# Feed-forward gate/up pairs as 2x2 block products with seven products, and SBUF handed out by phase

## The chip, the cores and the metric

The kernel runs on one core of one Trainium2 chip. The metric is the device time of one execution in microseconds (us). In the rows, PE is TensorE's matmuls and PEld its weight loads, DVE is VectorE, ACT ScalarE, POOL GpSimd, and SP SyncE, which issues the DMAs. In the code they are T, V, A, G and SP.

## The reference

Two layers of an encoder on 512 tokens of width 1024, float32. Each layer mixes the tokens in four ways, merges the four by gates, projects, adds the residual and normalises; then comes a feed-forward network of width 2816 (22 tiles of 128):

```python
for l in range(DEPTH):                       # DEPTH = 2
    h = x @ w_in[l]                          # q, k, v, gates of four token mixers
    ...                                      # retention, attention, GLA, S5 -> branches
    mixed = sum(sigmoid(x @ w_gate[l, b] + b_gate[l, b]) * (branches[b] @ w_branch[l, b]) for b in range(4))
    x = _layer_norm(DEEPNORM_ALPHA * x + mixed @ w_out[l], ln1_g[l], ln1_b[l])
    ffn = (silu(x @ w_ffn_gate[l]) * (x @ w_ffn_up[l])) @ w_ffn_down[l]
    x = _layer_norm(DEEPNORM_ALPHA * x + ffn, ln2_g[l], ln2_b[l])
```

## The kernel before

Every float32 product is made of three matmuls in the float32r type. `split` writes a value as a high part (a cast on ACT) and a low part (a subtraction on DVE), and `three` pairs high with high, high with low, low with high. The activations lie transposed in SBUF as XH and XL (128 partitions x 8 slices of the width x 512 tokens). A weight tile is loaded by SP into a ring `wr` of two buffers (`wload`) and split into the rings `wh` and `wl` of three.

In the gate/up stage `gemm_t` makes one tile of 128 outputs for all 512 tokens: 2 halves of 256 tokens x 3 pairs x 8 slices = 48 matmuls with 256 columns. Each of the 22 steps f makes a gate tile and an up tile, then silu on ACT, their product on DVE, and a split of that product g, which stays in SBUF for the down projection. `proj_ln` multiplies such split operands with the rows of a weight matrix, by 4 blocks t of 128 tokens, into eight PSUM banks, and calls `layer_norm` for each block as it becomes complete. `layer_norm` takes its square root as a power on POOL. Its `rest()` transposes a block on PE, applies scale and shift out of PSUM (ACT; DVE for half of the last block), and splits the result into XH and XL; the `rest()` of the last block is called inside the next stage's first matmuls (`late`). Its `rows()` applies scale and shift to the untransposed block on POOL, for the residual of the next normalisation.

Small tiles of 128x512 come from one pool: 53 slots of tag "a", 7 of "sg", 8 of "acc" (`BUFS`). PSUM has rings of 3 (`mm`) and 5 banks (`mx`). During layer 0's gate/up stage the state tables of layer 1's S5 mixer are also made (`s5_constants` on DVE, ACT and POOL, `s5_table` on POOL), and stored to DRAM (`esp`).

The order of the mixers' work is written by a planner (`Pace`, `run`) with costs of its own. The order of all instructions on each engine is made when the kernel is built, by priority (the order in the text, loads' splits ahead) and by when operands and buffers become free; on the chip each engine then works its list in order.

## Time and profile before

| | |
|---|---|
| time, 3 runs | median 1721.31 us (1719.19 to 1741.71) |
| profiled execution | 1720.08 us, span of instructions 1717.9 us |
| PE busy | 1651.2 us (96%) |
| DVE / ACT / POOL busy | 1000.2 / 613.4 / 353.4 us |
| gate/up stage, layer 0 and 1 | 499.8 to 748.4 us, 1343.3 to 1587.8 us |
| down projection of layer 0, to layer 1's start | 748.4 to 871.2 us |
| mean granted TensorE clock | 0.983 |

Shares of the span are means over stages with different limits, so a change in one stage is read from that stage's windows. Matmuls overlap: their cost is the distance of their starts, not the duration that a row shows. The time of the profiled execution holds some 2 us before the first and after the last instruction.

### The profile page before, as it was taken

To read this page: it belongs to the slowest core of one execution; us is meant where nothing else is said; L and a number is where in the kernel's file an instruction comes from. 1 tells how busy PE (TensorE), PEld (TensorE's weight loads), DVE (VectorE), ACT (ScalarE), POOL (GpSimd) and SP (SyncE) were. 2 spreads that over 40 slices of the span, in tenths; PEclk is the share of its full clock that TensorE was granted. 3 is DMA by queue.
4 is the path that set the end of the run, shared out by engine and by line. 5 is a ranking of instruction groups with operands and counts; after the bars stand their busy time and mean duration, and the time that the engine had idled before them with its cause. 6 is when DMAs were issued, how large, how long until landed. Compare 5 with 4: busy or idle time off the path is not lost. (4 is left out here: it accounts for less than half of the span.)

```text
span 1717.9 us, 27806 instructions
## 1 busy us (share of the span) xinstructions
PE 1651.2 (96%) x11596; PEld 1531.0 (89%) x11596; DVE 1000.2 (58%) x1473; ACT 613.4 (36%) x1012; POOL 353.4 (21%) x363
## 2 busy tenths in 40 slices
PE   8999998889999999999999999999999999999997
PEld 7989898779889999988889898988898899999886
DVE  4666579987586533322374665789865833333226
ACT  4454532233343222221154545433342522222112
POOL 0601024560038921000060000122300600000002
PEclk9998999899999999999999999999999999999999
DMA  6532212222433333322327332233324232222232
GB/s 200 176 111 76 86 62 94 82 82 99 141 99 99 123 123 117 119 98 98 111 74 259 104 96 92 64 117 125 125 93 160 86 102 96 99 99 99 98 99 74
DMA packets 66205, 186.94 MB, mean 109 GB/s; under 512 B 7136, under 2 KB 7328, under 8 KB 66080
## 3 DMA queue, kind: packets, MB, share of 16 engines
q1 hardware_dynamic: 66080, 185.17, 32.7%
q8 instruction: 91, 1.49, 0.4%
q14 instruction: 34, 0.28, 0.0%
HBM read 170.46 MB, written 14.68 MB: 108 GB/s over the span
## 5 line engine op out<-in xcount | busy, mean ns | idle before, releaser
L121 DVE TENSOR_TENSOR wl<-wr,wh 128x1024 fp32r<-128x1024 f32 (+2 forms) x250 | 317.3, 1270 | 440.9 <-ACT wh L121 427.0
L121 ACT CAST wh<-wr 128x1024 fp32r<-128x1024 f32 (+2 forms) x250 | 257.5, 1032 | 671.1 <-PE pg L121 223.6
L121 PE MATMUL pg<-XH,wh 128*128 128x256 f32 x2432 | 337.4, 281 | 2.2 <-DVE fs L121 2.2
L121 PE MATMUL pg<-XL,wh 128*128 128x256 f32 x2432 | 333.8, 280 | 2.5 <-DVE XL L121 2.5
L121 PE MATMUL pg<-XH,wl 128*128 128x256 f32 x2432 | 333.0, 280 | 0.0
L121 PEld LDWEIGHTS pg<-XH,wh 128*128 128x128 f32 x2432 | 312.1, 192 | 8.1 <-issue 3.1
L121 PEld LDWEIGHTS pg<-XL,wh 128*128 128x128 f32 x2432 | 306.0, 191 | 3.3 <-DVE XL L121 3.3
L121 PEld LDWEIGHTS pg<-XH,wl 128*128 128x128 f32 x2432 | 305.9, 191 | 0.4
L121 POOL TENSOR_TENSOR rs<-ve,ct 128x1 f32<-128x1 f32 x16 | 10.9, 682 | 718.2 <-DVE ve L121 718.2
L121 DVE TENSOR_TENSOR fs<-fs,pg 128x512 f32<-128x512 f32 x44 | 30.2, 687 | 159.5 <-PE pg L121 159.5
L121 PE MATMUL pj<-wl,gh 128*128 128x512 f32 x320 | 102.3, 393 | 0.0
L121 PE MATMUL pj<-wh,gl 128*128 128x512 f32 x320 | 101.8, 391 | 0.0
L121 PE MATMUL pj<-wh,gh 128*128 128x512 f32 x320 | 101.7, 391 | 0.0
L121 POOL TENSOR_TENSOR acc<-acc,sg 128x512 f32<-128x512 f32 x32 | 61.6, 1929 | 170.3 <-DVE sg L121 170.3
L121 PEld LDWEIGHTS pj<-wh,gh 128*128 128x128 f32 x320 | 59.9, 188 | 13.5
L121 PEld LDWEIGHTS pj<-wl,gh 128*128 128x128 f32 x320 | 60.1, 188 | 13.1
L121 PEld LDWEIGHTS pj<-wh,gl 128*128 128x128 f32 x320 | 60.1, 188 | 12.7
L121 PE MATMUL gn<-wh,XH 128*128 128x400 f32 (+1 forms) x128 | 49.1, 384 | 6.2 <-ACT XH L121 6.2
L121 POOL TENSOR_TENSOR hr<-hv,ct 128x8 f32<-128x8 f32 x8 | 13.2, 1648 | 192.0 <-DVE hv L121 192.0
L121 PE MATMUL pb<-brh,bwh 128*128 128x512 f32 x128 | 51.8, 404 | 0.0
L121 PE MATMUL pb<-brh,bwl 128*128 128x512 f32 x128 | 51.3, 401 | 0.0
L121 PE MATMUL pb<-brl,bwh 128*128 128x512 f32 x128 | 51.3, 401 | 0.0
...
## 6 DMA issues: line engine op xcount, KB each, us to landing
...
```

The source lines that it names most:

```text
L121: r = fn(out, *a, **kw)
```

## The change

Gate and up of one tile f are the two rows of a 2x2 block matrix; the two halves of the width (512 each) are its inner dimension, the two halves of the tokens (256 each) the columns of the right side. `ffn` makes the four blocks of the result with seven products of half the depth: each is 3 pairs x 4 slices = 12 matmuls with 256 columns, 84 a tile. Five small operations on DVE combine the products.

The left sides are the weights, of which four are sums. The weights are laid out on the host in a new order of blocks, 2048 columns a tile. SP loads the first 1024 columns into `s13` and all 2048 into `raw`; a DMA issued from POOL then adds a third block to both halves of `s13` where they lie (`accum_op`), which makes two of the four sums. The other two (`s24`) are additions on POOL. Three splits of 1024 columns and one of 512 follow. The right sides are differences of the blocks of x (`block_sums`, after the transposes, on POOL for token block 2 and on DVE for block 3); one lies in XH and XL in place of a block that is no longer read, three in a new pool of 6 pairs (`bp`), which the mixers use for attention's q, k and results. The first two tiles' products that need only the first two token blocks come ahead of the rest (`PRE`).

The large pool is opened and closed by phase: mixers and output projection (`MIXERS`), g (`HELD`), gate/up (`FFN`), down projection (`DOWN`), where a tile of a new phase waits for the tiles that had its addresses. g is held unsplit and split in the down projection. `rows()` is gone: `rest()` stores the normalised rows to DRAM, and `residual` loads them, with scale and shift on POOL, before the projection that needs them. The state tables move from the gate/up stage to the down projection (`tables`).

```diff
-BUFS = {"a": 53, "sg": 7, "acc": 8}
+MIXERS = {"a": 37, "sg": 7, "acc": 8}
+HELD = {"g": 22}
+FFN = {"raw": 2, "s24": 2, "fh": 2, "fl": 2, "wk": 4, "po": 6}
+DOWN = {"x": 10, "ap": 6, "ws": 8, "a": 6}
+WIDE = {"raw": 2048, "s24": 1024, "fh": 1024, "fl": 1024}
+PAIRS = 6
...
     sm = pool("sm", 2)
-    ap_ = pool("ap", 53)
+    bp = pool("bp", PAIRS)
+    lp = pool("lp", 1)
...
+    phases = []
+    def phase(name, tags):
+        st = ExitStack()
+        phases.append((st, st.enter_context(tc.tile_pool(
+            name=nm(name), bufs=1, reuse_waits="tile")), tags))
+    def close():
+        phases.pop()[0].close()
     def slot(s, dt=F32, tag="a"):
+        p, tags = next(x[1:] for x in phases if tag in x[2])
+        return p.tile([P, WIDE.get(tag, 512)], dt, tag=tag, name=nm(s), bufs=tags[tag])
+    def has(tag):
+        return any(tag in x[2] for x in phases)
+    def kept(s):
+        return lp.tile([P, 512], F32, tag=s, name=nm(s))
+    def pair(s):
         n = nm(s)
-        return ap_.tile([P, 512], dt, tag=tag, name=n, bufs=BUFS[tag])
+        return bp.tile([P, 1024], F32R, tag="b", name=n, bufs=PAIRS)
...
+    def split_pair(s, src):
+        x = pair(s)
+        split(x[:, 0:512], x[:, 512:1024], src)
+        return x[:, 0:512], x[:, 512:1024]
...
-        hs, ls = [slot("wsh", F32R) for _ in range(2)], [slot("wsl", F32R) for _ in range(2)]
+        tag = "ws" if has("ws") else "a"
+        hs, ls = ([slot(s, F32R, tag) for _ in range(2)] for s in ("wsh", "wsl"))
...
         def rest():
+            for h in range(2):
+                SP.dma_start(xsp[P * t:P * t + P, 512 * h:512 * h + 512], xh[h])
             tp = [mx_ps("tp") for _ in range(2)]
-            xf = [slot("xf") for _ in range(2)]
+            xf = [kept(f"xf{h}") if sums is not None and t == 1 else
+                  slot("xf", tag="g" if sums is not None and t == 3 else "a") for h in range(2)]
...
             for h in range(2):
-                split(XH[:, 4 * h:4 * h + 4, P * t:P * t + P], XL[:, 4 * h:4 * h + 4, P * t:P * t + P],
-                      xf[h].rearrange("p (k c) -> p k c", c=P))
-        def rows():
+                if sums is None or t < 2 or h == 1:
+                    split(XH[:, 4 * h:4 * h + 4, P * t:P * t + P],
+                          XL[:, 4 * h:4 * h + 4, P * t:P * t + P],
+                          xf[h].rearrange("p (k c) -> p k c", c=P))
+            if sums is not None:
+                block_sums(sums, t, xf)
+        return rest
...
+    def block_sums(sums, t, xf):
+        raw, parts = sums
+        raw.append(xf)
+        if t < 2:
+            return
+        e = G if t == 2 else V
+        (b11, b21), (b12, b22) = raw[t - 2], xf
+        t1, t2, t3, t4 = (slot("bs", tag="a" if t == 2 else "g") for _ in range(4))
+        cols = slice(P * (t - 2), P * (t - 2) + P)
+        for i, (o, a, b) in enumerate(((t1, b11, b12), (t3, b12, b22), (t2, b11, t3), (t4, b21, t2))):
+            e.tensor_tensor(o, a, b, ALU.subtract)
+            h, l_ = (x[:, :, cols] for x in parts[i])
+            split(h, l_, o.rearrange("p (k c) -> p k c", c=P))
+    def residual(l, which, src, scaled):
+        tag = "x" if has("x") else "a"
+        xh = [[kept(f"x{h}") if t == 3 else slot("x", tag=tag) for h in range(2)] for t in range(4)]
+        gb = None if scaled else ln_params(l, which, tag)
+        for t in range(4):
             for h in range(2):
-                G.tensor_tensor(xh[h], xh[h], gt[h], ALU.mult)
-                G.tensor_tensor(xh[h], xh[h], bt[h], ALU.add)
-        return rest, rows, power
-    def proj_ln(l, w_, lh, ll, nk, wsrc, kl, ks, xh, gt, bt, last):
+                SP.dma_start(xh[t][h], src[P * t:P * t + P, 512 * h:512 * h + 512])
+                if gb:
+                    G.tensor_tensor(xh[t][h], xh[t][h], gb[0][h], ALU.mult)
+                    G.tensor_tensor(xh[t][h], xh[t][h], gb[1][h], ALU.add)
+        return xh
...
+            if not isinstance(a[k], tuple):
+                tag = "ap" if k < 7 else "g"
+                a[k] = split_slots("ap", a[k], (tag, tag))
+            if also:
+                also(k)
...
             if t > 0 and not last:
-                todo[t - 1][0]()
-        def rows():
-            with tc.issue_after(todo[3][2].ins):
-                for x in todo:
-                    x[1]()
-        return todo[3][0], rows
-    def ln_params(l, which):
+                todo[t - 1]()
+        return todo[3]
...
+            x = pair("br")
+            brs_.append((x[:, 0:512], x[:, 512:1024]))
...
+    def ffn(l, parts, rest):
+        X = lambda k0, c0: [[x[:, k0 + k, c0:c0 + 256] for k in range(4)] for x in (XH, XL)]
+        b11, b21, b22 = X(0, 0), X(4, 0), X(4, 256)
+        t1, t3, t2, t4 = ([[x[:, k, :] for k in range(4)] for x in p] for p in parts)
+        def weights(f):
+            r = slot("raw", tag="raw")
+            s13 = wp.tile([P, 1024], F32, tag="wr", name=nm("ws"), bufs=2)
+            SP.dma_start(s13, wgu[l, f][:, 0:1024])
+            SP.dma_start(r, wgu[l, f])
+            nc.gpsimd.dma_start(s13.rearrange("p (a c) -> p a c", a=2),
+                                bc(wgu[l, f][:, 1024:1536].unsqueeze(1), [P, 2, 512]),
+                                accum_op=ALU.add)
+            h, l_ = (wp.tile([P, 1024], F32R, tag=t, name=nm(t)) for t in ("wh", "wl"))
+            split(h, l_, r[:, 0:1024])
+            hl = lambda h, l_: [(h[:, 512 * i:512 * i + 512], l_[:, 512 * i:512 * i + 512]) for i in range(2)]
+            w = {}
+            w[1], w[4] = hl(h, l_)
+            w[2] = split_slots("wk", r[:, 1536:2048], ("wk", "wk"))
+            s24 = slot("s24", tag="s24")
+            G.tensor_tensor(s24[:, 0:512], s13[:, 512:1024], r[:, 0:512], ALU.add)
+            G.tensor_tensor(s24[:, 512:1024], s24[:, 0:512], r[:, 1536:2048], ALU.add)
+            h, l_ = (slot(t, F32R, t) for t in ("fh", "fl"))
+            split(h, l_, s13)
+            w[7], w[5] = hl(h, l_)
+            h, l_ = (wp.tile([P, 1024], F32R, tag=t, name=nm(t)) for t in ("wh", "wl"))
+            split(h, l_, s24)
+            w[6], w[3] = hl(h, l_)
+            return w
+        def product(ps, w, x, first):
+            n = 0
+            for a, b in three((w, x)):
+                for k in range(4):
+                    T.matmul(ps, a[:, P * k:P * k + P], b[k], start=first and n == 0,
+                             stop=n == 11, skip_group_check=True)
+                    n += 1
+        def head(w):
+            pa = mx_ps("fa")[:, 0:256]
+            u = slot("fu", tag="po")
+            product(pa, w[1], b11, True)
+            A.copy(u[:, 0:256], pa)
+            return pa, u
+        def head2(w, pa):
+            product(pa, w[2], b21, False)
+            s = slot("fs", tag="po")
+            A.activation(s[:, 0:256], pa, AF.Silu)
+            return s
+        def tile_of(w, pa, u, s):
+            pb, pc = mx_ps("fb")[:, 0:256], mm_ps("fc")[:, 0:256]
+            y = slot("fy", tag="po")
+            p1, u2, p15 = u[:, 0:256], u[:, 256:512], y[:, 256:512]
+            product(pb, w[6], t2, True)
+            V.tensor_tensor(u2, p1, pb, ALU.subtract)
+            product(pc, w[5], t1, True)
+            V.tensor_tensor(p15, pc, p1, ALU.add)
+            if s is None:
+                s = head2(w, pa)
+            product(pb, w[7], t3, False)
+            V.tensor_tensor(p15, pb, p15, ALU.subtract)
+            product(pc, w[3], b22, False)
+            V.tensor_tensor(s[:, 256:512], pc, u2, ALU.add)
+            A.activation(s[:, 256:512], s[:, 256:512], AF.Silu)
+            product(pb, w[4], t4, False)
+            V.tensor_tensor(y[:, 0:256], pb, p1, ALU.subtract)
+            return s, y
+        ws, hs, ss, gs = {}, {}, {}, []
+        for f in range(PRE):
+            ws[f] = weights(f)
+            hs[f] = head(ws[f])
+            if f == 0:
+                rest()
+            if f:
+                ss[f - 1] = head2(ws[f - 1], hs[f - 1][0])
+        ss[PRE - 1] = head2(ws[PRE - 1], hs[PRE - 1][0])
+        for f in range(NF):
+            if f >= PRE:
+                ws[f] = weights(f)
+                hs[f] = head(ws[f])
+            s, y = tile_of(ws.pop(f), *hs.pop(f), ss.pop(f, None))
+            g = slot("g", tag="g")
+            V.tensor_tensor(g, s, y, ALU.mult)
+            gs.append(g)
+        return gs
+    s5c_ = [None]
+    def tables(k):
+        if k == 0:
+            s5c_[0] = s5_constants(1)
+        elif k % 2 == 0 and k <= 16:
+            for i, x in enumerate(s5_table(k // 2 - 1, s5c_[0][3])):
+                SP.dma_start(esp[k // 2 - 1, i], x)
     rest = None
     for l in range(L):
+        phase("mx", MIXERS)
         tt_ = lambda i, s: gemm_t(wt[l, i], s)
...
-            rows()
-            with tc.issue_after(wdma[0].ins):
-                for t in range(4):
-                    for h in range(2):
-                        SP.dma_start(xsp[P * t:P * t + P, 512 * h:512 * h + 512], xh[t][h])
+            s5c_[0] = s5_constants(0)
+        aq = [split_pair("aq", tt_(4 + i, "aq")) for i in range(2)]
+        ak = [split_pair("ak", tt_(6 + i, "ak")) for i in range(2)]
         brs = [[None, None] for _ in range(4)]
...
-        run(g_gate, attention(l, aq, ak, va, brs[1]), ret(), gl(), s5(l, s5c, uspr, brs[3]))
-        xh = [[slot("x") for _ in range(2)] for _ in range(4)]
-        for t in range(4):
-            for h in range(2):
-                src = xn if l == 0 else xsp
-                SP.dma_start(xh[t][h], src[P * t:P * t + P, 512 * h:512 * h + 512])
-        gt, bt = ln_params(l, 0)
-        rest, rows = proj_ln(l, 0, [m[0] for m in mix], [m[1] for m in mix], 8, wo[l], 4, 2, xh, gt, bt, False)
-        gt, bt = ln_params(l, 1)
-        ghs, gls = [], []
-        ps = gemm_ts([wgu[l, i] for i in range(3)], "pg", rest)
-        for f in range(NF):
-            if f > 0:
-                ps += [gemm_t(wgu[l, i], "pg") for i in range(max(3, 2 * f), 2 * f + 2)]
-            pg, pu = ps[2 * f:2 * f + 2]
-            if f == 1:
-                rows()
-            s = slot("fs")
-            A.activation(s, pg, AF.Silu)
-            V.tensor_tensor(s, s, pu, ALU.mult)
-            h, l_ = split_slots("g", s, ("acc", "acc") if f < 4 else ("sg", "sg") if f < 7 else ("a", "a"))
-            ghs.append(h)
-            gls.append(l_)
-            if l + 1 < L and f == 0:
-                s5c = s5_constants(l + 1)
-            if l + 1 < L and f % 2 == 0 and 4 <= f < 20:
-                j = f // 2 - 2
-                for i, x in enumerate(s5_table(j, s5c[3])):
-                    SP.dma_start(esp[j, i], x)
-        rest, rows = proj_ln(l, 1, ghs, gls, NF, wdn[l], 4, 2, xh, gt, bt, l == L - 1)
+        run(g_gate, attention(l, aq, ak, va, brs[1]), ret(), gl(), s5(l, s5c_[0], uspr, brs[3]))
+        xh = residual(l - 1, 1, xn if l == 0 else xsp, l == 0)
+        parts = [[x[:, 0:4, 256:512] for x in (XH, XL)]]
+        for _ in range(3):
+            parts.append([pair(x).rearrange("p (k c) -> p k c", c=256) for x in ("bh", "bl")])
+        rest = proj_ln(l, 0, mix, 8, wo[l], 4, 2, xh, None, None, False, ([], parts))
+        close()
+        phase("hd", HELD)
+        phase("ff", FFN)
+        gs = ffn(l, parts, rest)
+        close()
+        phase("dn", DOWN)
+        xh = residual(l, 0, xsp, False)
+        gt, bt = ln_params(l, 1) if l == L - 1 else (None, None)
+        rest = proj_ln(l, 1, gs, NF, wdn[l], 4, 2, xh, gt, bt, l == L - 1,
+                       also=tables if l + 1 < L else None)
+        close()
+        close()
...
     r["wo"] = a["w_out"].reshape(L, 8, P, D)
-    r["wgu"] = np.stack([_tiles(a["w_ffn_gate"]), _tiles(a["w_ffn_up"])], axis=2).reshape(L, 2 * NF, P, D)
+    g, u = _tiles(a["w_ffn_gate"]), _tiles(a["w_ffn_up"])
```

## Rows read from the trace of the kernel before

**Rows 1.** The page: busy us by engine; DMA queues (packets, MB, share).
```profile
PE 1651.2 (96%) x11596; PEld 1531.0 (89%) x11596; DVE 1000.2 (58%) x1473; ACT 613.4 (36%) x1012; POOL 353.4 (21%) x363
...
q1 hardware_dynamic: 66080, 185.17, 32.7%
q8 instruction: 91, 1.49, 0.4%
q14 instruction: 34, 0.28, 0.0%
```
**Rows 2.** Windows: both gate/up stages; a down projection; a stretch of loads; a stall.
```profile
core 0: us, PE busy (x) PEld busy (x) DVE busy (x) ACT busy (x) POOL busy (x), PEclk, DMA share, GB/s
499.80:748.40 248.60, 244.11 (x2130) 243.09 (x2129) 116.98 (x140) 77.91 (x107) 108.15 (x123) 0.99 0.36 117
1343.30:1587.80 244.50, 242.23 (x2129) 241.35 (x2128) 96.97 (x102) 77.78 (x105) 27.16 (x17) 1.00 0.31 102
748.40:871.20 122.80, 122.80 (x547) 100.75 (x545) 42.79 (x55) 31.74 (x46) 1.65 (x3) 1.00 0.27 90
...
910.00:920.00 10.00, 10.00 (x91) 10.00 (x90) 2.30 (x3) 3.07 (x4) 0.00 (x0) 1.00 0.81 304
...
528.00:532.00 4.00, 2.93 (x18) 2.96 (x19) 3.90 (x9) 1.57 (x2) 0.00 (x0) 0.77 0.19 50
532.00:536.00 4.00, 4.00 (x31) 4.00 (x31) 3.40 (x21) 1.84 (x4) 1.88 (x11) 0.81 0.59 212
```
**Rows 3.** Timeline of PE, layer 0: last gate/up matmuls, first of the down projection.
```profile
743.85 1.07 PE L121 MATMUL pg<-XL,wh 128*128 128x256 f32 x8
...
747.47 1.07 PE L121 MATMUL pg<-XH,wl 128*128 128x256 f32 x8
748.38 0.62 PE L121 MATMUL pj<-wh,gh 128*128 128x512 f32 x2
```
**Rows 4.** Groups by form: split and combining operations of DVE, ACT and POOL.
```profile
L121 ACT CAST wh<-wr 128x1024 fp32r<-128x1024 f32 x234 | 245.6, 1051 | 649.0 <-PE pg L121 211.3 <-issue 191.5 <-PE pj L121 171.4
...
L121 POOL TENSOR_TENSOR acc<-acc,sg 128x512 f32<-128x512 f32 x32 | 61.6, 1929 | 170.3 <-DVE sg L121 170.3
...
L121 DVE TENSOR_TENSOR gl<-fs,gh 128x512 fp32r<-128x512 f32 x44 | 36.3, 825 | 0.0
...
L121 DVE TENSOR_TENSOR fs<-fs,pg 128x512 f32<-128x512 f32 x44 | 30.2, 687 | 159.5 <-PE pg L121 159.5
...
L121 POOL TENSOR_TENSOR er<-ea,eb 128x512 f32<-128x512 f32 x16 | 18.6, 1163 | 45.6 <-DVE gl L121 25.9 <-DMA esp<-ei 18.4 <-PE ro L121 1.3
...
L121 DVE TENSOR_TENSOR gs<-gu,ct 128x256 f32<-128x256 f32 x16 | 6.2, 417 | 0.0
...
L121 ACT CAST v<-gn 128x256 fp32r<-128x256 f32 x16 | 5.7, 373 | 8.3 <-DVE v L121 5.8 <-PE gn L121 2.4
```
**Rows 5.** The large DVE subtraction, by form, in 640-748 us (POOL nearly idle).
```profile
L121 DVE TENSOR_TENSOR wl<-wr,wh 128x1024 fp32r<-128x1024 f32 x20 | 24.5, 1225 | 31.7 <-ACT wh L121 31.7
```
**Rows 6.** The same group in 520-600 us (POOL busy 71.4 of 80 us).
```profile
L121 DVE TENSOR_TENSOR wl<-wr,wh 128x1024 fp32r<-128x1024 f32 x15 | 23.0, 1531 | 11.2 <-ACT wh L121 11.2
```
**Rows 7.** Who waited for whom: the SyncE queue, first row.
```profile
SPq L121 <- DVE wl L121: 1296.9, 217, 19.5
```
**Rows 8.** Timeline, layer 1: from the output projection into the gate/up stage.
```profile
1348.55 2.91 DVE L121 TENSOR_SCALAR x<-x,mv,rs 128x512 f32<-128x512 f32 x2 [0.44 <-POOL rs L121]
...
1354.35 3.43 DVE L121 TENSOR_TENSOR XL<-xf,XH 128x512 fp32r<-128x512 f32 x2
...
1357.84 0.74 PE L121 MATMUL pg<-XL,wh 128*128 128x256 f32 x4 [0.96 <-DVE XL L121]
```
**Rows 9.** Timeline, layer 0: the stall behind the state-table constants.
```profile
522.71 5.35 DVE L121 TENSOR_SCALAR s5w<-s5w 128x72 f32<-128x72 f32 x5
...
529.07 1.16 PE L121 MATMUL pg<-XH,wh 128*128 128x256 f32 x8 [2.23 <-DVE fs L121]
```
**Rows 10.** The chain that ended last: one 256 KB load, issue to landing.
```profile
1344.67 3.84 DMA lg<-in_lng
```

21 lines of the change are left out of this document (10 added, 11 removed).

## The prediction

> **What bounds the kernel now.** Start at the page's line of engines [rows 1]: TensorE (PE) is busy 1651 of 1718 us, and no other engine passes 58%. Then go to the windows of the two gate/up stages [rows 2]: PE is busy in 244.1 of 248.6 us and in 242.2 of 244.5 us, while DVE works 117 and 97 us and ACT 78. So in the stage that changes, work taken from PE is time, as long as nothing else comes to need more than PE does per tile f. What one matmul costs is read from starts, since busy times of pipelined matmuls overlap: in the timeline at the end of layer 0's stage [rows 3] the starts at 743.85 and 748.38 us lie 5 groups of 8 apart, 113.3 ns each. A tile f has 96 such matmuls, 10.88 us; 22 tiles are 239.3 us. The stage takes 9.3 us more than that in layer 0 and 5.2 us more in layer 1 [rows 2], nearly all of it at its start. The loads are no bound: SyncE waits 1297 us in all for the subtraction that frees the buffer of raw weights [rows 7], so each load starts when a buffer is free, long before PE needs it.
>
> **The matmuls.** Seven products of 12 matmuls are 84, of the same form (128x128 weights, 256 columns), where there were 96. I take the same 113.3 ns, since the tile, the type and the one weight load per matmul stay: 9.52 us a tile, 1.36 us less, and over 44 tiles -59.8 us. This term is firm; all others take from it.
>
> **What each tile adds to the other engines.** DVE: three subtractions of 128x1024 and one of 128x512, where there were two of 128x1024 and, for g, one of 128x512. The large one takes 1225 ns with POOL idle [rows 5] and 1531 ns with POOL busy [rows 6]; POOL will be busy about a third of a tile, so 1.33 us, 4.0 for three; 0.75 for the 512 one (between 687 and 825 [rows 4]). Five combinations of 128x256 out of PSUM cost 417 each [rows 4], 2.1 in all, and the product s*y 0.69. Sum 7.5 us of 9.52, 79%, where it was 4.4 of 10.88. ACT: three casts of 1051 ns, one of half the size at about 0.6, three small ones of 373 [rows 4]: 4.9 us, 51%. POOL: two additions of 128x512 at 1.16 to 1.93 us [rows 4], 2.3 to 3.9, and the issue of the accumulating DMA. None of these sums passes PE's 9.52.
>
> **What they cost PE.** Because DVE is 79% busy and in order, PE will now and then wait for it. The tight place: p15 must be read out of pb after the product with w7 and before the one with w4, with only w3's 12 matmuls (1.36 us) between; a 1.33 us subtraction that has just begun and the 0.42 us of p15 itself are 1.75, so up to 0.4 us is exposed. The second: with three wh/wl buffers and two taken per tile, the pair (w6, w3) of the next tile can be split only once a pair of this tile is released, after w3 or w4. Cast and subtraction (1.05 + 1.33) then stand against 1.36 to 2.7 us of matmuls plus the 0.9 us by which the low half is needed later: nothing to 0.3 us. Floor 0 (PE can't go below its matmuls); ceiling 1.36 a tile, where the products gain nothing. I take 0.4 us, the first place's own figure, for 42 tiles: +17 us (0 to 57).
>
> **The DMAs.** A tile loads 1.5 MB (s13 and the raw 1 MB) where it was 1 MB. At 304 GB/s the DMA share was 0.81 [rows 2], so some 375 GB/s is full, and 1.57 million bytes are 4.2 us. For the accumulating DMA the trace has no row: the page has one queue of data and two of instructions, none from POOL [rows 1]. Occupancy: from 1.4 us (as a plain load of its 512 KB) to 2.8 (it reads source and destination); I take the upper, 7.0 of 9.52 us, so bandwidth hides. Landing: the nearest row is a 256 KB load spread over the partitions, 3.84 us [rows 10]; 512 KB lie between that and twice that, 7.7. I take 5, nearer the row. The load of s13, the DMA, POOL's two additions and the split follow each other, about 4 + 5 + 3 + 2.4 = 14 us for one tile; two buffers of s13 and raw let two tiles' chains overlap, a need of 7 us per tile, so it hides under 9.52. The Trainium skill, "DMA: Bandwidth & Descriptors", "Anatomy of one DMA — SWDGE (gpsimd) path", prices a DMA issued from GpSimd at about 2.0 us plus its bytes at 436 GB/s, an estimate of 3.2 us here, by which the chain is 12 us and the sum the same; no run shows it yet.
>
> **The start of the stage.** Before, the last token block's path (statistics, normalisation, transposes, splits) ends 14.5 us after the output projection's last matmul: 1343.3 to the last subtraction into XL, 1354.35 + 3.43 [rows 8]. It was slow because POOL scaled the rows beside it: its last normalising pair took 2.91. That scaling moves to the down projection, which saves some 3 us here, and two splits of XL fall away, 1.4. But block 2's four differences are split on DVE first (4 x 0.75 = 3.0), and of block 3's four (0.69 each, on DVE, after the transposes) three and their splits come before t2, which the first full product needs: 4.3. So t2 is there after about 17.4 us. PE meanwhile has only the four products that read the first two token blocks, 48 matmuls or 5.4 us. So the stage exceeds its matmuls by about 12 us in each layer, against 9.3 and 5.2: +9.5. In layer 0 the old excess holds another stall, 2.23 us behind the state-table constants on DVE [rows 9], after which the granted clock was 0.77 and 0.81 in two windows of 4 us [rows 2] (a part of each at 1.2 GHz, the rest at 2.4), some 1.7 us lost; layer 1 kept 1.00. A wait of 10 us will bring this to both: +2. Together +12, from -1 (t2 at 12 us) to +36: by phases, the raw tiles take addresses of mixer slots that the output projection's operands hold until its end, so the first 1 MB may start only there, some 6 us before the first product, and the following tiles' loads queue behind it.
>
> **The other moves.** The rows of the normalised x go to DRAM in each rest() and come back at the next projection: 8 stores and 8 loads of 256 KB, and 4 loads of scale and shift, on SyncE, in order with the weight loads; POOL's 16 operations of 1.16 to 1.93 us [rows 4], 19 to 31 us, hide under the down projection, which keeps PE busy without a gap for 122.8 us [rows 2]. The g splits move there too, with DVE at 1.33 + 0.75 us in each of 22 steps of 5.6 us. The state tables (48 such POOL operations, 56 us or more, with only four free slots) share the place and may reach its end, where the last normalisation's power stands on POOL: I put 2 us on layer 1's start and 1 on each down projection. The mixers have 37 + 12 small slots where they had 53: 3 us (from -5, since the early scaling on POOL leaves layer 1, to +20). Sum +7 (-5 to +25).
>
> **Sum.** -59.8 + 17 + 12 + 7 = -24 us on the profiled execution's 1720.1 (span 1717.9 and 2.2 around it), which is 1.2 below the median of the three runs: 1697.
>
> **Rivals.** First, all of it hides: 0.1 us of stall a tile, the start no longer than before, mixers unchanged: -59.8 + 4 - 1, so 1664. For it: DVE's sums stay under PE's; against it: the waits named are short of cover. Second, slower: POOL takes one tile's accumulating DMA, waits for it to land and adds, and only then issues the next, because its queue is in order. Issue (0.6, a guess, no row shows one), landing 3.84 to 7.7, two additions 2.3 to 3.9: 6.7 to 12.2 us a tile. From 9.9 it sets the pace, from 10.88 the stage is slower than before. With 11.5 us the stage costs 44 x 0.6 = +27, with starts and moves +19, and PE's repeated waits of 2 us a tile bring the lower clock as at 528 us, a few us more: about 1770. A rule of the Trainium skill says the same of such waits: "TensorE: Matmul & The Clock Gate", "HAM oscillation", has a loop fall back to half rate in each round by its DMA wait; rows 2 show this after 2.23 us of wait, and none after 0.96 in rows 8. Third, the phases make each border serial: loads and splits of a new phase wait for the old one's last users, 36 us at the starts and 15 elsewhere: -59.8 + 17 + 51, so 1729. That fewer matmuls run than said is not a case: the products are counted in the code.
>
> **How the numbers follow.** Forecast (1677 to 1715) 0.45; all hidden 0.19; serial borders 0.19; POOL's chain 0.17. A measurement tells some 2% from no change, here 1687 and 1756. Faster: all of the first rival and the forecast's part below 1687, 0.19: 0.38. Slower: nearly all of POOL's chain, 0.15. Same: 0.47. The range leaves out half of the upper rival and the floor of the lower: 1660 to 1752.
>
> **What will show it.** 3696 gate/up matmuls where 4224 were, at 113 ns; PE's starts in the middle of a stage 9.5 to 10.3 us a tile apart, with gaps in front of the products with w4 or w6, ended by DVE; DVE about 165 us busy per stage; a gap of 8 us or more within the first 20 us of each stage, ended by DVE's subtractions, with a lower clock behind it. POOL waiting for its own DMA in each tile, and PE then for B's split, would make the second rival right and me wrong; so would DMA shares near 1. PE idle ended by a load at a border speaks for the third.

## The result and the profile after

The changed kernel takes 1787.13 us (median of four runs, 1784.06 to 1790.67) where the kernel before takes 1720.25: the ratio, made from the means of the runs, is 1.036 [1.028, 1.045], slower. The prediction of 1697 us and its range are both missed, and on the wrong side. The profiled execution after took 1790.67 us, with a span of 1788.8 and a mean granted clock of 0.962.

Page of the kernel after: the engines' busy time, the DMA queues, two groups that the change made costly, and the new DMA's issues (the answer to [rows 1]).

```profile
PE 1641.2 (92%) x11068; PEld 1503.4 (84%) x11068; DVE 1224.6 (68%) x1801; ACT 711.1 (40%) x1200; POOL 550.4 (31%) x503
...
q1 hardware_dynamic: 70688, 216.63, 35.7%
...
q0 software_dynamic: 11968, 23.07, 7.5%
...
L126 PE MATMUL pj<-wh,aph 128*128 128x512 f32 x320 | 106.8, 409 | 39.4 <-ACT wh L126 37.1
...
L1084 POOL DMA_DIRECT2D ws<-in_wgu x44 | 52.9, 1213 | 81.5 <-DMA ws<-in_wgu 81.5
...
ws<-in_wgu POOLq DMA_DIRECT2D x44, 512.0 KB, 6.4
```

PE has 528 records fewer, as counted, but only 10 us less busy time, and its idle time grew from 67 to 148 us. So there are two losses: the matmuls did not become cheaper in proportion, and PE waits. The stages show where. Their bounds are starts in PE's timeline: the first matmul of the output projection, the transposes behind its last, the first of the down projection, the first projection of the next layer (872.0 us before; the 871.2 given ahead of the prediction are the transposes in front of it). The last column is the best version found below.

| stage, us | before | after | difference | e12 |
|---|---|---|---|---|
| mixers, layer 0 | 453.9 | 467.1 | +13.2 | 455.2 |
| output projection | 45.9 | 45.9 | 0 | 46.4 |
| gate/up, layer 0 | 248.6 | 245.9 | -2.7 | 242.9 |
| down projection, layer 0 | 123.6 | 177.1 | **+53.5** | 125.6 |
| mixers, layer 1 | 425.4 | 425.8 | +0.4 | 423.0 |
| output projection | 45.9 | 45.9 | 0 | 46.7 |
| gate/up, layer 1 | 244.5 | 249.4 | +4.9 | 240.7 |
| down projection, layer 1 | 121.1 | 122.3 | +1.2 | 123.8 |
| end | 9.1 | 9.3 | +0.2 | 9.3 |

Three quarters of the loss lie in a stage whose matmuls did not change. Layer 1's down projection, which has the same moves except the state tables, grew by 1.2 us only. Windows of the kernel after (columns as in [rows 2]): both gate/up stages, layer 0's down projection, the steady middle of a stage, and the hole in the down projection.

```profile
core 0: us, PE busy (x) PEld busy (x) DVE busy (x) ACT busy (x) POOL busy (x), PEclk, DMA share, GB/s
513.00:759.00 246.00, 227.84 (x1866) 225.74 (x1864) 187.03 (x246) 118.64 (x182) 100.23 (x73) 0.96 0.66 191
1407.80:1657.30 249.50, 226.86 (x1866) 225.09 (x1864) 194.76 (x247) 118.95 (x182) 102.85 (x69) 0.96 0.66 188
759.00:936.00 177.00, 136.02 (x551) 107.45 (x552) 80.71 (x115) 42.65 (x68) 100.22 (x121) 0.87 0.33 113
580.00:740.00 160.00, 160.00 (x1350) 160.00 (x1349) 121.30 (x162) 75.53 (x113) 68.20 (x47) 1.00 0.72 206
800.00:820.00 20.00, 3.90 (x14) 2.63 (x12) 1.74 (x1) 1.05 (x1) 18.51 (x40) 0.61 0.15 53
```

**The hole.** The same down projection kept PE busy without a gap before [rows 2]; now PE works 3.9 of 20 us while POOL is the only busy engine, and the granted clock is 0.61 (much of the window at 1.2 GHz). Over the whole stage PE is idle for 41.0 us, and busy 13.2 us longer than the 122.8 before, at a granted clock of 0.87. The page's group says that PE waits for ACT's cast of a weight tile, 37.1 us. ACT is idle too, so go on to the queue that loads the tile. SP's timeline and SP's waits (783 to 870 us) of the kernel after:

```profile
782.77 0.33 SPq L126 DMA_DIRECT2D wr<-in_wdn  x1
813.46 0.33 SPq L126 DMA_DIRECT2D esp<-er  x1
813.88 0.37 SPq L126 DMA_DIRECT2D wr<-in_wdn  x1
...
SPq L126 <- POOL er L126: 51.8, 8, 30.3
SPq L126 <- POOL ei L126: 25.1, 8, 4.9
```

Between 783.1 and 813.5 us SP issues nothing: it stands at the first store of a state table (`esp<-er`) until POOL has made that table. The loads of the down projection's weights (`wr<-in_wdn`) are behind that store in SP's queue. POOL is late since it first scales the residual's rows (766 to 792 us) and makes the tables' constants (792 to 808). Sixteen such stores take turns with the loads, and SP waits for POOL at each of them, 76.9 us in all.

**The steady stage.** From 580 to 740 us PE is busy in 160.00 of 160.00 us, at a granted clock of 1.00, with DVE at 76%; in layer 1 the same holds from 1480 to 1640 us. So no tile waits, and POOL's chain is hidden. But the tiles are too far apart. PE's timeline of the kernel after (answers to [rows 3]): two neighbouring groups of 4, twice, and the same product of two neighbouring tiles.

```profile
700.60 0.64 PE L126 MATMUL fc<-XH,fh 128*128 128x256 f32 x4
701.08 0.64 PE L126 MATMUL fc<-XL,fh 128*128 128x256 f32 x4
...
704.44 0.64 PE L126 MATMUL fb<-bh,fl 128*128 128x256 f32 x4
704.92 0.63 PE L126 MATMUL fc<-XH,wh 128*128 128x256 f32 x4
...
739.08 0.64 PE L126 MATMUL fb<-bh,wh 128*128 128x256 f32 x4
749.05 0.63 PE L126 MATMUL fb<-bh,wh 128*128 128x256 f32 x4
```

Four matmuls take 0.48 us, 120 ns each, and a tile takes 9.97 us, 118.7 ns for each of its 84 matmuls, where the same form cost 113.3 before [rows 3]. Seven products of 12 then save 0.91 us a tile, 40.0 in all.

**The start.** 22 tiles of 9.97 us are 219.4; the stages take 26.5 and 30.0 more than that, against 9.3 and 5.2 before. PE's, ACT's and SP's timelines at layer 0's start, after (answers to [rows 8] and [rows 9]), and the window:

```profile
513.04 1.04 PE L126 MATMUL tp<-ct,x 128*128 128x128 f32 x8
...
525.38 1.01 PE L126 MATMUL fa<-XH,wh 128*128 128x256 f32 x3 [11.31 <-ACT wh L126]
...
522.05 1.99 ACT L126 CAST fh<-ws 128x1024 fp32r<-128x1024 f32 x2
524.29 1.04 ACT L126 CAST wh<-raw 128x1024 fp32r<-128x1024 f32 x1 [0.25 <-DMA raw<-in_wgu]
...
486.94 4.72 SPq L126 DMA_DIRECT2D ws<-in_wgu  x2
...
497.96 21.09 SPq L126 DMA_DIRECT2D xsp<-x  x8
519.16 0.37 SPq L126 DMA_DIRECT2D raw<-in_wgu  x1
...
520.00:530.00 10.00, 2.61 (x10) 2.31 (x11) 10.00 (x9) 6.19 (x8) 6.59 (x4) 0.50 0.76 271
```

The first product waits 11.3 us behind the transposes. Its raw weights are asked for only at 519.2 us, behind eight stores of normalised rows that wait for the last normalisation. They land just before 524.3 us, when ACT is done with two other casts, too.

### The profile page after: what moved, and what is told of

The parts are those of the page before. It is cut to its first block, busy times and chain, and to the rows that moved or that the text cites. A ratio compares the mean times of both kernels' runs of the same rounds, so it can differ in the third digit from the quotient of the medians.

```text
span 1788.8 us, 27714 instructions
## 1 busy us (share of the span) xinstructions
PE 1641.2 (92%) x11068; PEld 1503.4 (84%) x11068; DVE 1224.6 (68%) x1801; ACT 711.1 (40%) x1200; POOL 550.4 (31%) x503
## 5 line engine op out<-in xcount | busy, mean ns | idle before, releaser
L126 DVE TENSOR_TENSOR wl<-wr,wh 128x1024 fp32r<-128x1024 f32 (+2 forms) x162 | 205.0, 1267 | 296.9 <-ACT wh L126 284.8
L126 PE MATMUL pg<-XH,wh 128*128 128x256 f32 x1024 | 150.1, 288 | 1.3 <-DVE sg L126 1.2
L126 PE MATMUL pg<-XL,wh 128*128 128x256 f32 x1024 | 146.9, 284 | 0.0
L126 PEld LDWEIGHTS pg<-XH,wh 128*128 128x128 f32 x1024 | 139.7, 196 | 8.5 <-DVE sg L126 2.6
L126 PE MATMUL pg<-XH,wl 128*128 128x256 f32 x1024 | 144.9, 282 | 0.0
L126 PE MATMUL pj<-wh,aph 128*128 128x512 f32 x320 | 106.8, 409 | 39.4 <-ACT wh L126 37.1
L126 PEld LDWEIGHTS pg<-XL,wh 128*128 128x128 f32 x1024 | 134.2, 194 | 1.0
L126 PEld LDWEIGHTS pg<-XH,wl 128*128 128x128 f32 x1024 | 132.0, 191 | 0.7
L126 PE MATMUL pj<-wh,apl 128*128 128x512 f32 x320 | 105.6, 404 | 4.4 <-DVE apl L126 4.4
L126 PE MATMUL pj<-wl,aph 128*128 128x512 f32 x320 | 105.1, 402 | 0.3 <-DVE wl L126 0.3
L126 PEld LDWEIGHTS pj<-wh,apl 128*128 128x128 f32 x320 | 62.0, 195 | 19.8 <-DVE apl L126 6.2
```

The lines of the kernel that those rows point to most:

```text
L126: r = fn(out, *a, **kw)
```

## The experiments

Ratios are to the kernel before. Edits are to the kernel after, unless said otherwise; "l0" and "l1" are the layers. In the tables' stores and the rows' stores, `pace.issue` keeps the planner's count as it was.

**e1_esp_pool: the tables' stores go to POOL's own queue.**

```diff
-                SP.dma_start(esp[k // 2 - 1, i], x)
+                nc.gpsimd.dma_start(esp[k // 2 - 1, i], x)
```

> The changed kernel, with the 16 stores of the state tables (layer 0's down projection) issued from POOL's queue in place of SP's. First theory: SP works its queue in order, so each store that waits for POOL's table holds up the loads of wdn queued behind it (37.1 and 14.3 us of SP's waits between 800 and 840 us, 14.7 and 10.8 us between 840 and 885 us). Then the down projection of layer 0 falls from 176 us to 123 to 132 us, TensorE's wait for a cast of wdn from 37.1 us to under 5, and the time from 1787 to 1733 to 1745 us. Rival: POOL itself, busy for 19 of 20 us in that stretch, holds the stage through the residual or the layer norm, or the loads wait for their buffers; then the time stays within 10 us of 1787, or grows by POOL's 16 issues of 1.2 us.

Measured: 1757.92 us, 1.020 [1.016, 1.024]. SP's waits for POOL are gone, PE's wait of 37.1 us for ACT has fallen to 1.2, and l0's down projection takes 144.3 us. So the queue's order was the cause of most of the hole; the size is -29 us. What is late next stands at the end of the stage, in the groups of the transposes (e1; the idle time and its end are the last columns):

```profile
L126 PE MATMUL tp<-ct,x 128*128 128x128 f32 x20 | 3.6, 334 | 11.9 <-DVE x L126 11.9
```

DVE normalises late because the square root's power on POOL stands behind the tables, which POOL finishes at about 887 us.

**e2_xsp_pool: the normalised rows' stores go to POOL's queue.**

```diff
-                SP.dma_start(xsp[P * t:P * t + P, 512 * h:512 * h + 512], xh[h])
+                nc.gpsimd.dma_start(xsp[P * t:P * t + P, 512 * h:512 * h + 512], xh[h])
```

> The changed kernel, with the eight stores of the normalised rows per layer norm issued from POOL's queue in place of SP's. First theory: these stores, which wait for VectorE one row tile after the other from 498.0 to 518.7 us, hold up the load of the first raw weights behind them on SP (issued at 519.2 us, though its buffers may have been free sooner). Then the raw load is issued near 507 us, the gap between the output projection's last matmul (513.0 us) and the first gate/up matmul (525.4 us) falls by 8 to 12 us, each of the two gate/up stages gets 8 to 15 us shorter, and the time comes to 1757 to 1772 us. Rival: the raw weights' buffers lie over tiles of the mixers and of the projection that are read until about 518 us, so that the load waits for those all the same; then the stages stay at 246 and 249 us and the time at 1782 to 1792 us.

Measured: 1787.3 us, 1.037 [1.033, 1.040]. The load comes earlier and nothing is won: the rival's outcome. SP's and ACT's timelines, e2:

```profile
512.77 12.59 SPq L126 DMA_DIRECT2D raw<-in_wgu  x2
...
522.80 0.62 ACT L126 CAST bh<-bs 128x512 fp32r<-128x512 f32 x1 [1.05 <-POOL bs L126]
523.33 1.99 ACT L126 CAST fh<-ws 128x1024 fp32r<-128x1024 f32 x2
525.22 1.04 ACT L126 CAST wh<-raw 128x1024 fp32r<-128x1024 f32 x1
```

The raw weights are asked for some 6 us sooner (512.8 against 519.2), but the cast that PE needs stands in ACT's list behind the cast of a block sum that POOL finishes at 522.8, and behind two casts for later products. The stores were one of two waits that end at nearly the same time.

**e3_shift64: a tile of 64 bytes per partition ahead of the gate/up stage's buffers.**

```diff
         phase("ff", FFN)
+        shift = phases[-1][1].tile([P, 16], F32, tag="shift", name=nm("shift"), bufs=1)
```

> The changed kernel, with 64 unused bytes per partition ahead of the buffers of the gate/up stage, so that the weight tiles fh, fl and wk begin at an address of 192 modulo 256, as wh and wl do, and no longer at 128, as the moving tiles do. First theory: the matmul pitch depends on how the weights lie to the moving operand: 120.0 ns for weights in fh, fl and wk and 117.7 for wh and wl in the changed kernel, against 113.3 in the kernel before. Then all products go to 113.3 ns, a tile takes 9.52 us in place of 9.97, and the time falls by 3696 x 5.4 ns = 20 us, to 1765 to 1770 us. Weaker form: fh, fl and wk fall to the 117.7 ns of the others, 4 us, 1783. Rival: the pitch follows from something else (the order of the products, the accumulating DMA's traffic); then it stays at 118.7 ns on the mean and the time within 3 us of 1787.

Measured: 1777.17 us, 1.032 [1.029, 1.036]. PE's timeline, e3, on both sides of short waits:

```profile
721.31 0.62 PE L126 MATMUL fb<-bl,wh 128*128 128x256 f32 x4
721.76 0.62 PE L126 MATMUL fb<-bh,wl 128*128 128x256 f32 x4
...
724.09 0.74 PE L126 MATMUL fb<-bh,wh 128*128 128x256 f32 x4 [0.35 <-ACT wh L126]
...
730.16 0.63 PE L126 MATMUL fb<-bh,fh 128*128 128x256 f32 x4
730.63 0.63 PE L126 MATMUL fb<-bl,fh 128*128 128x256 f32 x4
```

No product keeps the pitch of 120 ns. There are two levels instead: four matmuls take 0.45 us (113.3 ns each) ahead of 724 us and 0.47 us (117.8 ns) from 727 on. Of the distances below 125 ns, 77% in layer 0 are below 115.5 ns (mean 114.4), in layer 1 39% (mean 116.1). The profiled execution took 1787.87 us, the longest of the six, and its two stages are 6.5 us shorter than after. The weights in wh and wl and their moving operands did not move in this run, yet their products, at 117.7 ns in the kernel after, follow the same two levels; so the distance of the addresses, which the first theory goes by, is not all. The level changes where the even row of starts is broken: here mostly behind waits, in e12 behind a single distance of 128 ns (651.9 us).

**e4_no_accum: the two sums of the accumulating DMA as two more additions on POOL.**

```diff
-            SP.dma_start(s13, wgu[l, f][:, 0:1024])
             SP.dma_start(r, wgu[l, f])
-            nc.gpsimd.dma_start(s13..., bc(wgu[l, f][:, 1024:1536]...), accum_op=ALU.add)
+            for i in range(2):
+                cols = slice(512 * i, 512 * i + 512)
+                G.tensor_tensor(s13[:, cols], r[:, cols], r[:, 1024:1536], ALU.add)
```

> The changed kernel, with the two sums w1 + p and w4 + p added by POOL from the raw weights (two more 128x512 additions) in place of the separate load and the accumulating DMA. First theory: the accumulating DMA is hidden in the steady part, where TensorE is busy without a gap, and POOL's two more additions (about 1.5 us each, 6.6 us of a tile's 9.97 in all) are hidden as well; the tiles stay 9.97 us apart and the time within 8 us of 1787. First rival: the accumulating DMA (6.4 us to landing, behind a load on SP's queue) delays the starts of the stages; then the two stages get 5 to 15 us shorter in sum, 1772 to 1782. Second rival: POOL becomes the bound of a tile; then tiles come more than 10.3 us apart and the time goes above 1800.

Measured: 1811.39 us, 1.052 [1.049, 1.055]. The stages take 256.5 and 261.1 us, 22.3 more in all, though the load per tile falls by a third; steady tiles are 10.19 us apart. Groups of DVE between 600 and 740 us, e4 first, then the kernel after:

```profile
L126 DVE TENSOR_TENSOR wl<-raw,wh 128x1024 fp32r<-128x1024 f32 x14 | 27.7, 1977 | 0.0
L126 DVE TENSOR_TENSOR g<-fs,fy 128x512 f32<-128x512 f32 x14 | 25.0, 1789 | 0.0
```

```profile
L126 DVE TENSOR_TENSOR wl<-raw,wh 128x1024 fp32r<-128x1024 f32 x15 | 18.3, 1220 | 0.0
L126 DVE TENSOR_TENSOR g<-fs,fy 128x512 f32<-128x512 f32 x15 | 11.3, 756 | 0.0
```

POOL is now busy in 109.3 of 140 us and DVE in 130.9, and the same subtraction takes 1977 ns where it took 1220, the product 1789 where it took 756 (one other subtraction, `fl`, fell from 1440 to 1225); DVE was busy in 105.9 of 140 us in the kernel after. The time is the second rival's (above 1800), the tiles stay under its 10.3 us, and the cause that the rows suggest is not POOL's own pace but DVE's beside it; about half of the loss lies outside the steady tiles. Four matmuls on `fh` still take 0.48 us, so the accumulating DMA is not what makes the pitch of 120 ns. The Trainium skill, "SBUF — State Buffer", "Who interferes with whom", states that a DVE instruction with two inputs in SBUF and a POOL instruction that reads SBUF exclude each other; the direction of these rows agrees.

**e5_border: the gate/up loads' buffers in a pool of their own, the rows' stores off SP, block 2's sums on DVE, the first raw cast ahead of the others.**

```diff
-FFN = {"raw": 2, "s24": 2, "fh": 2, "fl": 2, "wk": 4, "po": 6}
+FFN = {"s24": 2, "fh": 2, "fl": 2, "wk": 4}
+LOADS = {"raw": 2, "po": 6}
...
-        e = G if t == 2 else V
+        e = V
...
+            if f < PRE:
+                with tc.issue_after(c.ins):     # c: the cast of r[:, 0:1024]
+                    split(h, l_, s13)
```

> The changed kernel with three things done at the border to the gate/up stage: the stores of the normalised rows on POOL's queue (as before, which alone gave nothing), the two raw buffers laid over the mixers' gate buffers, which are free from the projection on, and the order behind it: the block sums of the third row tile on VectorE in place of POOL, and the cast of w1 queued on ScalarE ahead of the cast of the accumulated sums. First theory: with the raw weights there, the start waits next in ScalarE's queue, behind the casts of the block sums (POOL's four subtractions, done at 522.8 us) and two casts of accumulated sums; then the first gate/up matmul comes 3 to 7 us sooner after the projection's last, the stages get 6 to 12 us shorter each, and the time is 1763 to 1776 us. Rival: what is late is the row sums themselves, which all but the first 48 products need; then the first matmul comes sooner and TensorE waits for VectorE's block sums instead, the stages lose at most 3 us each and the time stays above 1781.

Measured: 1779.88 us, 1.034 [1.031, 1.038]; the stages are 3.4 and 7.4 us shorter. PE's timeline, e5:

```profile
522.30 1.23 PE L127 MATMUL fa<-XH,wh 128*128 128x256 f32 x4 [9.04 <-ACT wh L127]
```

The wait ahead of the first product is 2.3 us shorter (9.04 for 11.31). Then DVE is close to its limit, busy in 29.3 of the 30 us from 520 on (29.4 in the kernel after): the splits and differences have to be made, whatever the order. That DVE alone is the bound there is not shown. The result lies between theory and rival.

**e6_esp_vres: e1, and the residual's scaling spread over eight steps on DVE.**

```diff
-                    G.tensor_tensor(xh[t][h], xh[t][h], gb[0][h], ALU.mult)
-                    G.tensor_tensor(xh[t][h], xh[t][h], gb[1][h], ALU.add)
+                    def scale(x=xh[t][h], h=h, e=G if later is None else V): ...
+                    scale() if later is None else later.append(scale)
...
+            if 8 <= k < 16:
+                later[k - 8]()
```

> The changed kernel with the table stores on POOL's queue (1758 us with that alone, where TensorE waited 11.9 us at the end of layer 0's down projection for the layer norm) and the 16 operations that scale the residual (26 us on POOL between 766 and 792 us) done by VectorE in the middle of the stage. First theory: the layer norm's power stands behind the tables in POOL's queue, and POOL ends them too late by those 26 us; then the wait at the end goes, the down projection of layer 0 falls from 144 to 124 to 130 us, and the time to 1737 to 1745 us. Rival: the end is late because VectorE runs slowly beside POOL (2.3 us for an operation in that stretch); then 16 operations more make VectorE later still and the time stays at 1752 to 1765 us.

Measured: 1746.51 us, 1.014 [1.011, 1.018]; l0's down projection 134.7 us. The way is the first theory's, but both figures stay above its ranges (124 to 130 us, 1737 to 1745); what is left are DVE's subtractions beside POOL's tables at the end (e6, groups between 845 and 870 us):

```profile
L126 DVE TENSOR_TENSOR wl<-wr,wh 128x1024 fp32r<-128x1024 f32 x5 | 15.6, 3139 | 7.2 <-ACT wh L126 7.2
```

**b1_shift64 and b2_shift32: the kernel before, with nothing changed but addresses.** Unused tiles of 64 bytes per partition ahead of the large pools (b1), of 32 ahead of XH and 96 behind (b2).

```diff
     hb = cp.tile([P, L, 36], F32, name="hb")
+    cp.tile([P, 16], F32, name="shift")
```

> The kernel before, with 64 unused bytes per partition ahead of the weight buffers, so that wh and wl lie at 0 modulo 128 as the moving tiles XH and XL do, and no longer at 64. First theory: equal addresses modulo 128 of weights and moving operand cost 6.7 ns for each matmul of 256 columns. Then the pitch of the gate/up products goes from 113.3 to 120.0 ns, these stages get 4224 x 6.7 ns = 28 us longer, the 2784 such matmuls of the mixers up to 19 us, and the time goes from 1720 to 1748 to 1768 us. Rival: the pitch has nothing to do with the address; then the time stays within 4 us of 1720.

> The kernel before, with XH and XL moved by 32 bytes against the weight buffers (the distance of their starts is 32 modulo 128 in place of 64). Theory one: only equal addresses modulo 128 cost, so that the pitch stays 113.3 ns and the time within 4 us of 1720. Theory two: the lines of 64 bytes that are read at one time must differ, and with 32 bytes each moving read straddles two; then the pitch rises, to 120 ns at most, and the time by up to 28 to 47 us. A pitch below 113.3 ns, and a time below 1710, would say that neither is the whole rule.

Measured: b1 1748.33 us, 1.015 [1.012, 1.019]; b2 1754.36 us, 1.019 [1.016, 1.022]. PE's timelines, b1 and then b2 (answers to [rows 3]):

```profile
700.45 1.11 PE L121 MATMUL pg<-XH,wh 128*128 128x256 f32 x8
701.40 1.11 PE L121 MATMUL pg<-XL,wh 128*128 128x256 f32 x8
```

```profile
701.11 1.12 PE L121 MATMUL pg<-XH,wh 128*128 128x256 f32 x8
702.07 1.12 PE L121 MATMUL pg<-XL,wh 128*128 128x256 f32 x8
```

Eight matmuls take 0.95 us in b1 and 0.96 in b2; from 580 to 740 us the means are 118.7 ns (single distances 115 to 122) and 120.0 ns (115 to 125). Every engine has the same instructions in the same order as before. The gate/up stages go from 248.6 and 244.5 us to 257.1 and 257.5 in b1, 259.2 and 257.5 in b2. So the pitch hangs on addresses. The first theory, that equal addresses modulo 128 cost, gives b1's direction at a smaller size, but not b2's rise; there the second theory's outcome came, and its mechanism, lines of 64 bytes, is not shown by any run.

**e7_all: e5, e6 and e3's shift together.** No edit beside theirs.

> The changed kernel with the mended parts together: table stores on POOL's queue and the residual scaled by VectorE (41 us by itself), the weight tiles of the gate/up stage moved by 64 bytes (10 us), the border of e5 (8 us). First theory: these are three separate causes at three places, and their gains add: 1787 - 41 - 10 - 8 = 1728 us, 1722 to 1736. Rival: they are covers of one another (a faster pitch only makes the border's VectorE work, or POOL, the bound), and the time stays above 1740.

Measured: 1728.23 us, 1.003 [1.001, 1.005]. The gains add: gate/up 234.9 and 241.3 us, l0's down projection 132.2.

**b3_slots41: the kernel before with 41 small slots.**

```diff
-BUFS = {"a": 53, "sg": 7, "acc": 8}
+BUFS = {"a": 41, "sg": 7, "acc": 8}
```

> The kernel before with 41 of the mixers' buffers in place of 53, near to what the change leaves them (37, and 12 halves of pairs that stay with a few tiles). First theory: layer 0's mixers are 13 us longer after the change (453.9 to 467.1 us) because a missing buffer shifts work in time; then they come to 460 to 470 us here, layer 1's to 425 to 432, and the time to 1727 to 1745 us. Rival: the number of buffers has no part in it, and the mixers stay within 3 us of 453.9.

Measured: 1734.44 us, 1.010 [1.006, 1.013]. l0's mixers take 463.5 us (+9.6) and l1's 425.7 (+0.3); nothing else changes. So fewer slots alone can cost most of the +13.2 us in l0's mixers; 41 are near to what the change leaves (37, and 12 halves of pairs), not the same.

The next five build on e7.

**e8_early: constants made in the gate/up stage, from its tile 4 on, tables in the first 16 steps of the down projection.**

```diff
+            if f == 4 and l + 1 < L:
+                s5c_[0] = s5_constants(1, (kept("xf0"), kept("xf1")))
...
-        elif k % 2 == 0 and k <= 16:
-            for i, x in enumerate(s5_table(k // 2 - 1, s5c_[0][3])):
+        if k < 16 and k % 2 == 0:
+            for i, x in enumerate(s5_table(k // 2, s5c_[0][3])):
```

> The kernel with all the mended parts, and POOL's 16 us of constants for the state tables moved out of the down projection of layer 0 into the gate/up stage (in buffers that are idle there), so that the tables begin with the stage. First theory: in that down projection the tables still end some 15 us too late, at 872 us, after the 858 at which the layer norm wants POOL, and slow VectorE's last subtractions; then the stage goes from 134.7 us to 123 to 127 us and the time is 8 to 12 us under that of all mended parts, 1714 to 1724, at or just under the kernel before (1720). Rival: POOL's constants lengthen VectorE's operations in the gate/up stage as POOL's sums did, and the time is that of all mended parts or more.

Measured: 1779.62 us, 1.034 [1.032, 1.036], a miss. The gate/up stage takes 253.6 us (234.9 in e7) and the down projection 166.7 (132.2), so both halves of the move cost. A group of DVE between 766 and 832 us, e8:

```profile
L127 DVE TENSOR_TENSOR apl<-g,aph 128x512 fp32r<-128x512 f32 x9 | 24.3, 2728 | 0.1
```

With POOL's tables back to back, a DVE operation of 128x512 takes 2728 ns, and PE waits 33.8 us for the split of g. Here POOL at full pace takes more from the kernel than POOL that is late.

**e9_vtab: the tables' products on DVE** (`e.tensor_tensor` with V for G in `s5_table`), the constants left on POOL.

> The kernel with all the mended parts, with the 48 operations of the state tables (POOL: 1.05 to 1.30 us each) done by VectorE in place of POOL, in the down projection of layer 0. First theory: what is left there (132 us against 122 in layer 1) is VectorE slowed by POOL beside it: its subtractions of 128x512 take 1.4 to 2.7 us where POOL works without a gap, 0.69 us where it doesn't. Then 48 x 0.69 = 33 us more on VectorE still make the stage shorter, 122 to 127 us, and the time falls by 5 to 10 us against that of all mended parts (1728), to 1716 to 1724. Rival: VectorE's own load decides (105 us busy of 135 in that stage already), and the added 33 us make the stage as long or longer: 1726 or more.

Measured: 1735.09 us, 1.006 [1.003, 1.009], a miss. The same groups between 780 and 830 us, e9:

```profile
L127 DVE TENSOR_TENSOR apl<-g,aph 128x512 fp32r<-128x512 f32 x11 | 7.5, 689 | 0.0
...
L127 DVE TENSOR_TENSOR er<-ea,eb 128x512 f32<-128x512 f32 x8 | 5.5, 688 | 11.8 <-POOL ea L127 11.8
```

DVE's operation is back at 689 ns, which bears out e8's reading; but DVE, in order, now stands 11.8 us at the first table, for POOL's constants, and PE waits 10.8 us for the split of g behind it. Neither theory is fully right.

**e10_lp: e9, with four of the mixers' small tiles in buffers that stand unused at that time.**

```diff
-            nb = slot("nb")
+            nb = kept(f"x{p}")
...
-        dt = slot("dt")
+        dt = kept("xf1")
...
-        c_f, cc, t_ = slot("scf"), slot("scc"), slot("sct")
+        c_f, cc, t_ = slot("scf"), kept("xf0"), slot("sct")
```

> The kernel of the tables on VectorE, with four long-lived tiles of the mixers (two bias tiles of the attention, the decay table of the retention, one coefficient tile of the state mixer) in the four buffers that the change holds aside for the block sums and the last row tile and that are idle in the mixers. First theory: the mixers' 13 us (453.9 to 467.1 us in layer 0; 463.5 in the kernel before with 41 buffers) are a matter of buffers, so four buffers more give back 4 to 10 us there, and the time is 1708 to 1717 us, under the kernel before (1721). Rival: the change ties the buffers to a few tiles and it isn't their number; then the mixers stay at 464 to 467 us and the time within 4 us of the kernel of the tables on VectorE.

Measured: 1725.62 us, 1.001 [0.998, 1.003]; l0's mixers 458.3 us, from 464.5 in e9. The mixers give the 4 to 10 us that were expected; the time, 9.5 us below e9, stays above the expected 1708 to 1717.

**e11_spread: e10, with the constants in parts over the gate/up stage's tiles, each part behind POOL's sums of a tile, and the tables from step 4 on.** `s5_constants` yields between its parts:

```diff
+            if f >= 2 and l + 1 < L:
+                with tc.issue_after(sums[0].ins):
+                    s5c_[0] = next(cs, None) or s5c_[0]
```

> The kernel of the four more buffers, with the constants of the state tables (16 us of small operations on POOL) spread over the tiles of layer 0's gate/up stage, a few behind each tile's sums, so that nothing of them is left in the down projection. First theory: there the tables on VectorE stood in its queue ahead of the splits of the products and waited 11.8 us for POOL's constants, and TensorE 10.8 us behind them; with the constants done, the down projection goes from 136 us to 123 to 127 us, the gate/up stage stays within 3 us, and the time falls by 9 to 13 us to 1711 to 1718, under the kernel before. Rival: it is VectorE's load that decides there, or POOL's small operations delay the sums in the gate/up stage as they did when they stood together (253.6 us in place of 234.9); then the time stays above 1722.

Measured: 1743.22 us, 1.011 [1.006, 1.016], a miss. l0's down projection falls to 125.6 us, as expected, but gate/up takes 271.9. POOL's timeline and a window, e11:

```profile
660.40 1.27 POOL L127 TENSOR_TENSOR s<-ws,raw 128x512 f32<-128x512 f32 x1 [6.96 <-issue]
667.42 1.21 POOL L1096 DMA_DIRECT2D ws<-in_wgu  x1
675.71 1.26 POOL L127 TENSOR_TENSOR s<-ws,raw 128x512 f32<-128x512 f32 x1 [7.08 <-issue]
...
660.00:700.00 40.00, 31.54 (x215) 30.25 (x215) 21.52 (x28) 12.99 (x20) 24.31 (x29) 0.83 0.49 139
```

The parts stand between one tile's sums and the issue of the next accumulating DMA, so a tile of POOL's chain takes 15.3 us (660.40 to 675.71) and PE waits for it: the second rival's mechanism, made by some microseconds of POOL's work in the wrong place.

**e12_behind: e11, with each part behind the issue of the DMA, not ahead of it (and from tile 3 on).**

```diff
-                with tc.issue_after(sums[0].ins):
+                with tc.issue_after(d.ins):     # d: this tile's accumulating DMA
```

> The kernel with the constants spread, with each tile's few constants queued on POOL behind the issue of that tile's accumulating DMA (in the 4 to 6 us in which POOL waits for its landing) in place of ahead of the next issue. First theory: POOL's chain of a tile (issue 1.2 us, landing about 5.5, two sums 2.6 to 3.5) takes 9.3 to 10.2 us, just what a tile takes on TensorE, so that the 5 to 7 us of constants ahead of the next issue made tiles 14 to 15 us long (660.4 to 675.7 us) and the stage 272 us; behind the issue they cost nothing. Then layer 0's gate/up stage comes back to 233 to 241 us, its down projection stays at 124 to 127, and the time is 1704 to 1716 us, under the kernel before. Rival: it isn't the place in POOL's queue but the small operations of VectorE and ScalarE that come with the constants (and ScalarE's changes of table), and the stage stays above 250 us, the time above 1725.

Measured: **1712.53 us, 0.994 [0.992, 0.996]**: 0.6% less than the kernel before, a small gain; its interval excludes 1. l0's gate/up stage takes 242.9 us, just above the expected 233 to 241. The same window, and l0's down projection, e12:

```profile
660.00:700.00 40.00, 40.00 (x356) 40.00 (x354) 29.90 (x44) 19.75 (x30) 25.17 (x32) 1.00 0.81 229
744.40:870.00 125.60, 124.01 (x552) 101.58 (x553) 93.81 (x141) 42.70 (x66) 13.85 (x25) 1.00 0.47 161
```

PE does not wait in the window, and the granted clock is 1.00. The parts now fill the time in which POOL waits for its DMA to land (6.0 us here).

## Why the prediction was wrong

By its terms, the sum of the measured ones, -40.0 + 0 + 42.0 + 68.5 = +70.5 us, is the difference of the spans (1788.8 - 1717.9 = 70.9) up to rounding.

- **The other moves, +7: measured +68.5, and here the prediction failed.** The step reads "The state tables ... share the place and may reach its end: ... I put 2 us on layer 1's start and 1 on each down projection". It asked what POOL's lateness costs at the end of the stage, and counted the tables' POOL operations. It did not count the 16 DMAs that the moved step issues, on SP, ahead of the weight loads. The kernel before had the same stores in a stage where loads had slack and POOL was early; moved behind 26 us of scaling and 16 of constants on POOL, the first one stopped SP for 30.3 us. e1 shows the queue (-29 us), e6 the scaling on POOL, e9 to e12 the constants; in e12 the stage is at 125.6 us of the old 123.6. The mixers' term (3 us) was off in size only: +13.2 in layer 0, of which b3 gives up to 9.6 to the number of slots. Its own bound of +20 held.
- **The matmuls, -59.8, called firm: measured -40.0.** The count was right; the price was taken as a property of the form. b1 and b2 show that the form costs 113.3, 118.7 or 120.0 ns by its buffers' addresses alone, and SBUF by phase moves them. e3 gives back half of the difference (about 10 us of 19.8).
- **What the tiles cost PE, +17: measured 0.** PE waits for nothing between 580 and 740 us, so the cover was enough; a tile of 9.97 us instead of 9.52 gave it more. It is enough without that, too: in e7 most tiles of layer 0 are 9.52 us apart. DVE's 76% came near the predicted 79%, and the accumulating DMA is hidden as said, though its landing took 6.4 us where 5 were taken, and its issue 1.21 where 0.6 was guessed. The Trainium skill's "DMA: Bandwidth & Descriptors", "Anatomy of one DMA — SWDGE (gpsimd) path", by which the estimate was 3.2 us, gives half of what was measured.
- **The starts, +12: measured +42.0**, just over the upper end and near the third rival's 36. That the first load comes late was named in the upper end, by the phases; in the kernel after it stands behind the stores on SP, and with these on POOL (e2) it still waits until 512.8 us, for their landing. But the terms were taken one by one, while three waits end within 3 us of each other: POOL's last block sum (521.5 us), ACT's two casts ahead (524.0), and the landing of the raw load (524.3). DVE is busy in 29.4 of the 30 us from 520 on besides. That e2, which took away only one of them, won nothing, and e5, which changed three, won 10.8 us in both layers, fits this. For the clock, 2 us were put; it was granted at 0.85 on the mean from 513 to 580 us, with PE idle for 17.0 us, and no run separates what each of the two cost.
- **The rivals.** The third named the borders and came nearest in kind; it gave 15 us to the moves elsewhere and kept the pitch, so its 1729 was too low as well. The second, POOL's chain, did not occur in the kernel after; that its 1770 lies nearest to the measured time is chance. e11 shows how little is missing to it. No rival had SP's queue.
- **What would show it:** 3696 matmuls and starts 9.97 us apart (9.5 to 10.3 said) came as said, 113 ns did not; DVE is busy 187 and 195 us per stage, where about 165 was said: in the steady part a tile takes 7.6 and 8.0 us of DVE, near the 7.5 said, and the work at the start comes on top. The gap came, too, but ACT's cast behind a load ended it, not DVE.

What the change is worth at its best is seen in e12: the two gate/up stages take 483.6 us instead of 493.1, the two down projections 249.4 instead of 244.7, and the whole kernel 0.6% less. The start keeps most of what the products save: e7's layer 0, with its tiles 9.52 us apart, takes 234.9 us, 25.5 more than its 22 tiles, where the kernel before took 9.3 more. What stays open is why PE's pitch moves between 113.3 and 117.8 ns at one and the same address distance (e3, e7), and whether another layout of the buffers would hold the lower one through both stages; it wasn't tried.
